# Attention's outputs kept with dimensions on partitions: square sums by a matmul with ones, roots in rows

## The chip, the cores and the metric

The kernel runs on one core of a Trainium2 chip. The metric is device time in microseconds of one execution. A core has TensorE (PE, matmuls; PEld is its weight load), VectorE (DVE), ScalarE (ACT), GpSimd (POOL) and SyncE (SP), which here issues nearly all DMAs. Matmuls read on-chip memory of 128 partitions and write PSUM, eight banks of 128 x 512 words.

## The reference

One block of a hybrid decoder on x (1 x 1024 x 1024): a norm, one combined projection, two groups of heads side by side, an output projection added to x, a last norm.

```python
h = rmsnorm(x, norm1_w)
proj = h @ w_in                       # 4104 columns: sb_q k v z (512 each), g_q k v z (512 each), g_b, g_a
o_sb = stick_breaking_attention(q, k, v)          # 8 heads of 64
o_sb = rmsnorm(o_sb, sb_norm_w) * silu(sb_z)      # a norm per head and position
o_gdn = gated_delta_chunked(gq, gk, gv, decay, beta)  # 4 heads of 128, a scan over chunks
o_gdn = rmsnorm(o_gdn, gdn_norm_w) * silu(g_z)
x = x + concat([o_sb, o_gdn]) @ w_out
out = rmsnorm(x, final_norm_w)
```

Stick-breaking attention gives key s the weight sigmoid(z_ts) times the product of (1 - sigmoid(z_tj)) over the keys j between s and t. So each row needs a scan. What matters here is the line of `o_sb`: every head's 64 outputs at a position are scaled by one over the root of their mean square, and by a gate.

## The kernel before

Products in float32 are made of float32r parts: a high part, and a low part that holds the rest. A product is then three matmuls (`mm3`, line 586).

The work is written as streams, Python generators that issue instructions (`Stream`, line 426, and `interleave`, line 440). While the program is built, a planner with a cost for each kind of instruction plays the streams forward and fixes the order of every engine: TensorE runs the instructions in the order in which the streams issued them, and the other engines in the order in which the planner saw them ready, by priority. So the order on the chip is fixed; an instruction that is late holds up what stands behind it on its engine. A stream gives way at every `yield`; yielding an instruction waits for it in the plan, yielding a function waits until it is true.

Streams by priority on TensorE: the delta rule (`delta_scan`, `delta_solve`, `delta_substitute`, `delta_pre`), the preparation and the weights of the output products, the attention windows, and as filling the projections (priority 100) and the output products.

- **Projections** (line 885). `ORDER`, line 29, is their order: G0 to G3 are a delta head's three projections (k, q, v), k0 to k3 keys of two attention heads each, z0 to z3 the gates of attention, z4 to z7 those of the delta heads, v1 values. Each projection is two halves of 24 matmuls of 512 columns. Its weights come by two loads, are split by ACT and POOL, and the result is evacuated by ACT and DVE and stored to DRAM. Gates and keys have their dimensions on partitions and positions along the row.
- **Delta rule** (lines 960 to 1248). Heads follow one another. A head's pre-stage needs its projections from DRAM, POOL substitutes forward, TensorE finishes the inverse with narrow matmuls (32 and 64 columns of weights), and the scan runs over eight chunks. It ends with the scale factors `rsg`. When the last is there, the weights of the output projection are loaded (line 1388).
- **Attention** (lines 1254 to 1363). For each of eight heads there are four windows of 256 positions (`window`, line 1287): scores, sigmoids on ACT, a scan on DVE, a product on POOL, transposes, and the weighted values into the bank `po`. This bank holds 128 rows by 256 positions: rows 0 to 63 come from the values' high parts, 64 to 127 from their low parts. ACT copies it to `o2`, two transposes put positions on partitions, a DVE reduction adds both halves, and the 256 x 64 outputs go to `o_s`, positions first. In the profile o2 appears as `o2f` and `otf`.
- **Output products** (lines 1404 to 1562). `enter_delta` and `enter_attention` load a block of 128 positions and its gates (`mgf`) and apply the norms. For attention this means a square on ACT, a reduction and a scaling on DVE, a root on POOL, and a multiplication. `prepare` and `split` transpose the block (four transposes, `mwf`), multiply it by the gates and split it into `mh` and `ml`. `products_delta` and then `products_attention` run 24 matmuls or more a block; the last also makes the final norm and stores.

Of the kernel before, what the change touches and what calls it, by code (L numbers as in the profile page):

```python
# [473 lines left out]
def block(tc, xT_d, x_d, n1_d, wE_d, wQ_d, wC_d, conv_d, alog_d, dtb_d, mixw_d, wo_d, fnw_d, out_d):  # L474
# [4 lines left out]
    with ExitStack() as top:  # L479
# [6 lines left out]

        fx = Fixed(ck, nc, {**{f"sg{w}": (2048 * (w + 1), 1) for w in range(4)}, "o2": (1024, 1), "kq": (4096, 4)})
        cst = open_pool("cst")
# [41 lines left out]
        g_s = dr.tile([GH, 3, P, T], F32, name="g_s")  # L530
        o_s = dr.tile([NB, P, 512], F32, name="o_s")
        og_s = dr.tile([NB, P, GH, P], F32, name="og_s")
# [14 lines left out]
        s0 = open_pool("s0", ctx=s0_ctx)  # L547
        n1 = s0.tile([P, NK], F32, name="n1")
        rbc = s0.tile([P, T], F32, name="rbc")
# [11 lines left out]
        class Columns:  # L561
# [629 lines left out]
        def gdn_chain(h, g):  # L1191
# [7 lines left out]
            for j in range(4):  # L1199
# [3 lines left out]
                if c == 0:  # L1203
                    xc = nkv[:, 0, :]
                else:
                    TE.matmul(ks, kq[:, j, 0, :], s_prev, start=True, stop=True)
                    xc = gd.tile([P, P], F32, tag="xct", bufs=2, name="xct")
                    yield V.scalar_tensor_tensor(xc, ks, gsc["neg"][:, h, c:c + 1], nkv[:, j, :], ALU.mult, ALU.add)
# [3 lines left out]
                if c < NB - 1:  # L1212
                    v2 = gd.tile([P, P], F32, tag="v2", bufs=2, name="v2")
                    r = V.tensor_scalar(v2, tx, r2k[:, j:j + 1], None, ALU.mult)
# [72 lines left out]
        def window(h, w, tok):  # L1287
# [30 lines left out]
            for j in range(w + 2):  # L1318
# [44 lines left out]
            yield  # L1363
# [43 lines left out]

        def split(pool, mg, gt):
            tp = pz()
            mw = fx.words(mg, "mw")  # L1410
            yield from turned(tp, [mw[:, 0, j * P:(j + 1) * P] for j in range(4)])
            fv = pools[0].tile([P, 512], F32, tag="mf", name="mf")
            V.tensor_tensor(fv, tp, gt.rearrange("p k t -> p (k t)"), ALU.mult)
            ck.free(mg)
            mh, ml = [pool.tile([P, 4, P], F32R, tag=f"m{c}", bufs=3, name=f"m{c}") for c in "hl"]
            A.activation(mh.rearrange("p k t -> p (k t)"), fv, AF.Copy)
            r = G.tensor_tensor(ml.rearrange("p k t -> p (k t)"), fv, mh.rearrange("p k t -> p (k t)").bitcast(F32), ALU.subtract)
            ck.hold(mh, ml)
            return mh, ml, r
# [32 lines left out]
        def prepare(g):  # L1452
            for b in range(NB):
                yield lambda: ("in", b, g) in ready and (b < 3 or f"{'ad'[g]}{b - 3}" in flags) and (b > 2 or g or f"d{5 + b}" in flags)
                mg, gt, r = ready["in", b, g]
                yield r
                yield lambda: ps.room("pz", 4)
                ready[b, g] = yield from split(pools[0], mg, gt)
                yield
# [20 lines left out]
        def products_delta():  # L1480
            for b in range(NB):
                for got in product(b, 1, (slice(0, 512), slice(512, D))):
# [8 lines left out]
                    yield  # L1491

        def enter_attention():
            yield lambda: "pool1" in flags and "z3" in flags and 3 in wts
            f0, f1 = pools[0], pools[1]
            for b in range(NB):
                yield lambda: f"e{SBH - 1}{b // 2}" in flags and ("in", NB - 1, 1) in ready and fx.room("kq")
# [12 lines left out]
                ready["in", b, 0] = mg, gt, V.tensor_tensor(o, o, rs.unsqueeze(2).to_broadcast([P, SBH, SBD]), ALU.mult)  # L1510
                yield

        def products_attention():
            yield lambda: f"d{NB - 1}" in flags
            for b in range(NB):
# [3 lines left out]
                for got in product(b, 0, parts):  # L1519
# [7 lines left out]
                    V.tensor_tensor(y[:, hs], yp, y[:, hs], ALU.add)  # L1527
                    junk = pools[1].tile([P, 568], F32, tag="yj", name="yj")
                    if n == 2:
# [39 lines left out]
                    Stream(enter_delta(), 9.3, OUTPUT), Stream(prepare(1), 9.2, OUTPUT), Stream(products_delta(), 101, OUTPUT),  # L1569
                    Stream(enter_attention(), 9.1, OUTPUT - 3), Stream(prepare(0), 9.05, OUTPUT - 2), Stream(products_attention(), 102, OUTPUT - 1.5)])  # L1570

# [37 lines left out]
```

## Time and profile before

| | |
|---|---|
| median of 3 runs | 647.9 us (647.87 to 647.94) |
| profiled execution | 648.05 us |
| its span | 646.3 us |
| TensorE busy, granted clock | 637.6 us, 0.998 |
| DVE, ACT, POOL busy | 425.0, 394.1, 339.3 us |
| DMA | 111.82 MB, mean 173 GB/s |

The profile is one execution. Its busy shares are averages over stages: up to about 85 us the first projections, then attention, delta rule and projections side by side up to about 546, then output products. Matmuls overlap their ends, so the distance between the starts of two neighbours, and not the duration of one, is what a matmul takes. All instructions are recorded through one helper and have its line, L358; they are told apart by the names of their tiles.

### The profile page before, as it was taken

How to read it: one execution, taken by the hardware profiler on the slowest of the kernel's cores; microseconds unless marked ns; L12 is line 12 of the kernel's file. 1: busy time of each engine (PE TensorE's matmuls, PEld its weight loads, DVE VectorE, ACT ScalarE, POOL GpSimd, SP SyncE). 2: the span in 40 equal slices, each digit the busy share in tenths (PEclk: the TensorE clock that was granted, in tenths of full speed). 3: DMA queues.
4: the chain of work that ended last, by engine and by line, in shares of the span. 5: the costliest groups of instructions: out<-in, count | busy, mean ns of one | idle time of the engine just before them, and what ended most of it. 6: DMA issues, size and time to landing. Idle time of an engine off the chain costs nothing.

```text
span 646.3 us, 11666 instructions
## 1 busy us (share of the span) xinstructions
PE 637.6 (99%) x3976; PEld 549.7 (85%) x3976; DVE 425.0 (66%) x779; ACT 394.1 (61%) x945; POOL 339.3 (53%) x428
## 2 busy tenths in 40 slices
PE   8999999999999999999999999999999999999996
PEld 7889988988888898888988888988888887888885
DVE  4469974223897768887658777585774237468864
ACT  5764577724968778787668677586654342132553
POOL 0115056837793668974496955668432232136632
PEclk9999999999999999999999999999999999999999
DMA  8886338866472553654345733636222279773123
GB/s 298 323 280 227 132 118 284 275 201 211 140 228 86 159 182 93 218 160 144 118 148 141 244 110 121 203 101 190 85 62 86 83 244 320 287 227 99 65 102 126
DMA packets 96666, 111.82 MB, mean 173 GB/s; under 512 B 28576, under 2 KB 61536, under 8 KB 96608
## 3 DMA queue, kind: packets, MB, share of 16 engines
q1 hardware_dynamic: 96320, 110.89, 53.0%
q8 instruction: 31, 0.51, 0.3%
q14 instruction: 27, 0.22, 0.1%
q10 hardware_dynamic: 288, 0.20, 0.1%
HBM read 76.03 MB, written 35.03 MB: 172 GB/s over the span
## 4 chain that ended last, share of the span: by engine, by line
PE 94%; DVE 2%; ACT 1%; issue 1%; POOL 1%; DMA 1%; POOLq 0%; SPq 0%; DVEq 0%; ACTq 0%
PE pp L358 55%; PE pz L358 27%; PE po L358 8%; PE pc L358 3%; DVE mgf L358 1%; POOL rsb L358 1%; DMA mgf<-gate_s 0%; DVE ssb L358 0%; DVE xr L358 0%; DVE mf L358 0%; ACT xinv L358 0%; ACT sgf L358 0%; DMA xr<-x 0%; DVE wol L358 0%; ACT nkv L358 0%
## 5 line engine op out<-in xcount | busy, mean ns | idle before, releaser
L358 PE MATMUL pp<-xh,weh 128*128 128x512 f32 x360 | 147.9, 411 | 0.0
L358 PE MATMUL pp<-xh,wel 128*128 128x512 f32 x360 | 141.5, 393 | 0.0
L358 PE MATMUL pp<-xl,weh 128*128 128x512 f32 x360 | 140.8, 391 | 0.0
L358 POOL TENSOR_TENSOR sgf<-sgf,cc 128x128 f32<-128x128 f32 (+3 forms) x64 | 77.3, 1210 | 56.8 <-DVE cc L358 52.5
L358 POOL TENSOR_TENSOR wel<-wer,weh 128x512 fp32r<-128x512 f32 x48 | 62.5, 1305 | 74.5 <-ACT weh L358 71.7
L358 PEld LDWEIGHTS pp<-xh,wel 128*128 128x128 f32 x360 | 67.6, 188 | 15.3
L358 PEld LDWEIGHTS pp<-xl,weh 128*128 128x128 f32 x360 | 67.8, 188 | 10.8
L358 PEld LDWEIGHTS pp<-xh,weh 128*128 128x128 f32 x360 | 67.6, 188 | 10.9 <-DVE ac L358 0.2
L358 DVE TENSOR_TENSOR_SCAN cc<-pz,step 128x384 f32<-128x384 f32 (+2 forms) x64 | 53.6, 848 | 13.1 <-ACT pz L358 9.5
L358 DVE TENSOR_TENSOR al<-pz,ah 128x512 fp32r<-128x512 f32 (+1 forms) x80 | 49.7, 632 | 18.9 <-ACT ah L358 18.5
L358 ACT ACTIVATE ah<-pz 128x512 fp32r<-128x512 f32 (+1 forms) x80 | 43.7, 565 | 24.1 <-PE pz L358 23.8
L358 ACT ACTIVATE sgf<-pz,rs 128x384 f32<-128x384 f32 (+3 forms) x96 | 54.5, 600 | 4.9 <-PE pz L358 4.6
L358 ACT ACTIVATE pz<-pz,ns 128x384 f32<-128x384 f32 (+3 forms) x96 | 53.2, 583 | 0.0
L358 PE MATMUL pp<-woh,mh 128*128 128x512 f32 (+2 forms) x132 | 51.9, 393 | 0.6 <-DMA mgf<-gate_s 0.5
L358 PE MATMUL pp<-woh,ml 128*128 128x512 f32 (+2 forms) x132 | 50.9, 385 | 0.0
L358 PE MATMUL pp<-wol,mh 128*128 128x512 f32 (+2 forms) x132 | 50.6, 384 | 0.0
L358 PE MATMUL po<-ah,v2a 128*128 128x256 f32 (+1 forms) x160 | 43.9, 300 | 0.0
L358 POOL TENSOR_TENSOR ml<-mf,mh 128x512 fp32r<-128x512 f32 x16 | 21.6, 1348 | 42.3 <-ACT mh L358 37.7
L358 DVE TENSOR_TENSOR_SCAN cc<-pz,cc,step 128x512 f32<-128x512 f32 (+1 forms) x32 | 38.8, 1213 | 6.7 <-ACT pz L358 5.8
L358 POOL TENSOR_TENSOR ac<-ac,pre 128x512 f32<-128x512 f32 x24 | 31.1, 1294 | 19.1 <-ACT pre L358 12.9
L358 DVE SCALAR_TENSOR_TENSOR pp<-pre,conv,pp 128x512 f32<-128x512 f32 x42 | 31.5, 751 | 13.6 <-ACT pp L358 13.0
L358 PE MATMUL po<-al,v2a 128*128 128x256 f32 (+1 forms) x160 | 38.7, 280 | 0.0
(292 smaller groups left out, 1591.5 us busy)
## 6 DMA issues: line engine op xcount, KB each, us to landing
wer<-wE SPq DMA_DIRECT2D x48, 256.0 KB, 3.6
xr<-x SPq DMA_DIRECT2D x16, 512.0 KB, 7.2
g_s<-ac SPq DMA_DIRECT2D x24, 256.0 KB, 2.4
v_s<-v2e SPq DMA_DIRECT2D x16, 256.0 KB, 2.4
kqf<-g_s SPq DMA_DIRECT2D x16, 256.0 KB, 3.5
v2a<-v_s SPq DMA_DIRECT2D x8, 512.0 KB, 4.3
q<-qk_s SPq DMA_DIRECT2D x8, 512.0 KB, 5.2
kh<-qk_s SPq DMA_DIRECT2D x8, 512.0 KB, 4.9
```

The source lines that it names most:

```text
L358: ins = f(*args, **kw).ins
```

## The change

A window no longer transposes its outputs. ACT copies the lower half of the bank (the low parts' share) to 64 partitions of `o2`, DVE adds the upper half, and the sum, 64 dimensions by 256 positions, is stored as it is. ACT squares it, the squares are split into a float32r high part and a rest on the other 64 partitions (ACT, POOL), and one matmul with a column of ones adds all 128 rows: the head's square sums in one row, which DVE copies and SP stores to `ss_s`.

A new stream, `attention_norms`, loads all sums as 64 rows of 128, makes one over the root on DVE (`_rsqrt`, line 48), and stores them to `rn_s`. `enter_attention` loads outputs and gates with dimensions on partitions, and each head's factors broadcast over its 64 partitions by two loads, and multiplies the gates by them. `split` does not transpose attention's blocks any more: it multiplies outputs by gates directly.

The order of projections becomes "... k1 k2 G2 G3 z4 k3 z5 ..." instead of "... k1 G2 k2 G3 k3 z4 z5 ...". Some buffers are made smaller (`xct`, `v2`, `junk`), `o2` gets a second one, `n1` is padded, and a column of ones is made at the start on ACT.

```diff
-ORDER = "G0 v1 k0 G1 k1 G2 k2 G3 k3 z4 z5 z6 z7 z0 z1 z2 z3".split()
+ORDER = "G0 v1 k0 G1 k1 k2 G2 G3 z4 k3 z5 z6 z7 z0 z1 z2 z3".split()
...
+        oner = cst.tile([P, 1], F32R, name="oner")
+        nc.scalar.activation(oner, half[:, 0:1], AF.Copy, scale=-2.0)
...
+            ts = slice(256 * w, 256 * w + 256)
+            yield lambda: fx.room("o2")
             o2 = fx.tile([P, 256], F32, "o2", "o2")
-            yield A.activation(o2, ov[:, 0:256], AF.Copy)
+            ck.hold(o2)
+            up, o = o2[0:64], o2[64:128]
+            A.activation(up, ov[64:128, 0:256], AF.Copy)
+            yield V.tensor_tensor(o, ov[0:64, 0:256], up, ALU.add)
             busy["po"] = 0
-            op = pz()
-            ot = fx.words(o2, "ot")
-            for i in range(2):
-                TE.transpose(op[:, i * P:(i + 1) * P].bitcast(F32R), ot[:, i * P:(i + 1) * P], idr)
-            oe = at_.tile([P, 2, SBD], F32, tag="oe", bufs=2, name="oe")
-            V.tensor_reduce(oe, op[:, 0:256].rearrange("p (i u d) -> p i d u", i=2, u=2), AX.X, ALU.add)
-            flags[f"e{h}{w}"] = S.dma_start(o_s[2 * w:2 * w + 2, :, h * SBD:(h + 1) * SBD].rearrange("b t d -> t b d"), oe)
+            A.activation(up, o, AF.Square)
+            yield lambda: at_.room("oe", 1)
+            sq = at_.tile([P, 256], F32R, tag="oe", name="sq")
+            ck.hold(sq)
+            A.activation(sq[0:64], up, AF.Copy)
+            r = G.tensor_tensor(sq[64:128], up, sq[0:64].bitcast(F32), ALU.subtract)
+            S.dma_start(o_s[h // 2, (h % 2) * 64:(h % 2) * 64 + 64, ts], o)
+            yield r
+            sp = pz()
+            TE.matmul(sp[0:1, 0:256], oner, sq, start=True, stop=True)
+            V.tensor_copy(o2[0:1], sp[0:1, 0:256])
+            flags[f"e{h}{w}"] = S.dma_start(ss_s[h:h + 1, ts], o2[0:1])
+            ck.free(o2, sq)
...
-        def split(pool, mg, gt):
-            tp = pz()
-            mw = fx.words(mg, "mw")
-            yield from turned(tp, [mw[:, 0, j * P:(j + 1) * P] for j in range(4)])
+        def split(pool, mg, gt, g):
             fv = pools[0].tile([P, 512], F32, tag="mf", name="mf")
-            V.tensor_tensor(fv, tp, gt.rearrange("p k t -> p (k t)"), ALU.mult)
+            if g:
+                tp = pz()
+                mw = fx.words(mg, "mw")
+                yield from turned(tp, [mw[:, 0, j * P:(j + 1) * P] for j in range(4)])
+                V.tensor_tensor(fv, tp, gt.rearrange("p k t -> p (k t)"), ALU.mult)
+            else:
+                V.tensor_tensor(fv, mg[:, 0, :], mg[:, 1, :], ALU.mult)
...
+        def attention_norms():
+            yield lambda: "pool0" in flags and all(f"e{SBH - 1}{w}" in flags for w in range(4))
+            nt = pools[0].tile([P, 3, P], F32, tag="sq", name="nt")
+            nv, rn, un = [nt[0:64, n, :] for n in range(3)]
+            S.dma_start(nv, ss_s.rearrange("h (b t) -> (h b) t", b=NB))
+            V.tensor_scalar(nv, nv, 1.0 / SBD, EPS, ALU.mult, ALU.add)
+            _rsqrt(V, None, rn, nv, P, un)
+            flags["rn"] = S.dma_start(rn_s.rearrange("h (b t) -> (h b) t", b=NB), rn)
...
-                S.dma_start(mx, o_s[b])
+                S.dma_start(mx.rearrange("p (k t) -> p k t", k=4), o_s[:, :, bs].rearrange("k p t -> p k t"))
                 ck.hold(mg)
-                S.dma_start(gt, gate_s[0:4, :, b * P:(b + 1) * P].rearrange("k e t -> e k t"))
-                o = mx.rearrange("p (h d) -> p h d", d=SBD)
-                sq = f0.tile([P, 512], F32, tag="sq", name="sq")
-                A.activation(sq, mx, AF.Square)
-                ss = f0.tile([P, SBH], F32, tag="ssb", name="ssb")
-                V.tensor_reduce(ss, sq.rearrange("p (h d) -> p h d", d=SBD), AX.X, ALU.add)
-                rs = f0.tile([P, SBH], F32, tag="rsb", name="rsb")
-                V.tensor_scalar(ss, ss, 1.0 / SBD, EPS, ALU.mult, ALU.add)
-                rsqrt(rs, ss, SBH)
-                ready["in", b, 0] = mg, gt, V.tensor_tensor(o, o, rs.unsqueeze(2).to_broadcast([P, SBH, SBD]), ALU.mult)
+                S.dma_start(gt, gate_s[0:4, :, bs].rearrange("k e t -> e k t"))
+                rb = f1.tile([P, 4, P], F32, tag="wr", bufs=2, name="rb")
+                for u in range(2):
+                    S.dma_start(rb[64 * u:64 * u + 64], rn_s.rearrange("(k u) t -> u k t", u=2)[u, :, bs].partition_broadcast(64))
+                ready["in", b, 0] = mg, gt, V.tensor_tensor(gt, gt, rb, ALU.mult)
```

More of the change, by code (lines that the diff above doesn't have):

```diff
@@ L485, in open_pool @@
             return Pool(ck, ctx.enter_context(tc.tile_pool(name=name, bufs=1, **kw)), space, before)
-        fx = Fixed(ck, nc, {**{f"sg{w}": (2048 * (w + 1), 1) for w in range(4)}, "o2": (1024, 1), "kq": (4096, 4)})
+        fx = Fixed(ck, nc, {**{f"sg{w}": (2048 * (w + 1), 1) for w in range(4)}, "o2": (1024, 2), "kq": (4096, 4)})
         cst = open_pool("cst")
@@ L530, in block @@
         g_s = dr.tile([GH, 3, P, T], F32, name="g_s")
-        o_s = dr.tile([NB, P, 512], F32, name="o_s")
+        o_s = dr.tile([SBH // 2, P, T], F32, name="o_s")
+        ss_s = dr.tile([SBH, T], F32, name="ss_s")
+        rn_s = dr.tile([SBH, T], F32, name="rn_s")
         og_s = dr.tile([NB, P, GH, P], F32, name="og_s")
@@ L547, in block @@
         s0 = open_pool("s0", ctx=s0_ctx)
-        n1 = s0.tile([P, NK], F32, name="n1")
+        n1 = s0.tile([P, 64], F32, name="n1")[:, 0:NK]
         rbc = s0.tile([P, T], F32, name="rbc")
@@ L1206, in gdn_chain @@
                     TE.matmul(ks, kq[:, j, 0, :], s_prev, start=True, stop=True)
-                    xc = gd.tile([P, P], F32, tag="xct", bufs=2, name="xct")
+                    xc = gd.tile([P, P], F32, tag="xct", bufs=1, name="xct")
                     yield V.scalar_tensor_tensor(xc, ks, gsc["neg"][:, h, c:c + 1], nkv[:, j, :], ALU.mult, ALU.add)
@@ L1212, in gdn_chain @@
                 if c < NB - 1:
-                    v2 = gd.tile([P, P], F32, tag="v2", bufs=2, name="v2")
+                    v2 = gd.tile([P, P], F32, tag="v2", bufs=1, name="v2")
                     r = V.tensor_scalar(v2, tx, r2k[:, j:j + 1], None, ALU.mult)
@@ L1455, in prepare @@
                 mg, gt, r = ready["in", b, g]
-                yield r
-                yield lambda: ps.room("pz", 4)
-                ready[b, g] = yield from split(pools[0], mg, gt)
+                if g:
+                    yield r
+                    yield lambda: ps.room("pz", 4)
+                ready[b, g] = yield from split(pools[0], mg, gt, g)
                 yield
@@ L1495, in enter_attention @@
             f0, f1 = pools[0], pools[1]
+            yield lambda: "rn" in flags
             for b in range(NB):
-                yield lambda: f"e{SBH - 1}{b // 2}" in flags and ("in", NB - 1, 1) in ready and fx.room("kq")
+                yield lambda: ("in", NB - 1, 1) in ready and fx.room("kq")
+                bs = slice(b * P, (b + 1) * P)
                 mg, mx, gt = block_inputs()
-                S.dma_start(mx, o_s[b])
+                S.dma_start(mx.rearrange("p (k t) -> p k t", k=4), o_s[:, :, bs].rearrange("k p t -> p k t"))
                 ck.hold(mg)
-                S.dma_start(gt, gate_s[0:4, :, b * P:(b + 1) * P].rearrange("k e t -> e k t"))
-                o = mx.rearrange("p (h d) -> p h d", d=SBD)
-                sq = f0.tile([P, 512], F32, tag="sq", name="sq")
-                A.activation(sq, mx, AF.Square)
-                ss = f0.tile([P, SBH], F32, tag="ssb", name="ssb")
-                V.tensor_reduce(ss, sq.rearrange("p (h d) -> p h d", d=SBD), AX.X, ALU.add)
-                rs = f0.tile([P, SBH], F32, tag="rsb", name="rsb")
-                V.tensor_scalar(ss, ss, 1.0 / SBD, EPS, ALU.mult, ALU.add)
-                rsqrt(rs, ss, SBH)
-                ready["in", b, 0] = mg, gt, V.tensor_tensor(o, o, rs.unsqueeze(2).to_broadcast([P, SBH, SBD]), ALU.mult)
+                S.dma_start(gt, gate_s[0:4, :, bs].rearrange("k e t -> e k t"))
[3 more added lines that the diff above has]
+                ready["in", b, 0] = mg, gt, V.tensor_tensor(gt, gt, rb, ALU.mult)
                 yield
@@ L1527, in products_attention @@
                     V.tensor_tensor(y[:, hs], yp, y[:, hs], ALU.add)
-                    junk = pools[1].tile([P, 568], F32, tag="yj", name="yj")
+                    junk = pools[1].tile([P, 560], F32, tag="yj", name="yj")
                     if n == 2:
```

3 lines of the change are left out of this document (2 added, 1 removed).

## The prediction

> **What bounds the kernel now.** I read the page's busy table and the chain of waits first, then TensorE's waits, then the busy time by stretches.
>
> ```profile
> PE 637.6 (99%) x3976; PEld 549.7 (85%) x3976; DVE 425.0 (66%) x779; ACT 394.1 (61%) x945; POOL 339.3 (53%) x428
> PE 94%; DVE 2%; ACT 1%; issue 1%; POOL 1%; DMA 1%; POOLq 0%; SPq 0%; DVEq 0%; ACTq 0%
> PE pp L358 <- DMA mgf<-gate_s: 0.5, 1, 0.5
> PE pz L358 <- DVE al L358: 0.2, 1, 0.2
> 165.00:500.00 335.00, 334.71 (x2386) 290.46 (x2385) 248.95 (x450) 241.15 (x648) 217.86 (x286) 1.00 0.48 144
> 500.00:546.00 46.00, 46.00 (x229) 38.47 (x227) 19.49 (x39) 16.73 (x35) 13.55 (x14) 1.00 0.66 217
> 546.00:640.00 94.00, 93.44 (x450) 76.96 (x448) 64.13 (x112) 38.25 (x73) 37.77 (x31) 1.00 0.45 153
> ```
>
> The first line is each engine's busy time, the second the chain by engine: TensorE is both the busiest engine and the path. The two waits are all that the profile shows of it standing still after the start. The last three rows are stretches (length, then busy time of PE, weight load, DVE, ACT, POOL): attention beside the delta rule and the projections, the end of the projections, the output products. TensorE fills 334.71 of 335, 46 of 46 and 93.44 of 94 us. The program's TensorE order is fixed when it is built, and other engines have room. So I count the change in TensorE time, start to start, and ask of everything else only whether it is still covered.
>
> **Removed from TensorE: 64 transposes in the windows.** Timeline of TensorE, start and duration of one (durations overlap; only the distance of starts is cost):
>
> ```profile
> 175.12 0.29 PE L358 MATMUL pz<-step,otf 128*128 128x128 f32 x2
> 175.25 0.35 PE L358 MATMUL po<-ah,v2a 128*128 128x256 f32 x1
> 175.44 0.28 PE L358 MATMUL po<-al,v2a 128*128 128x256 f32 x1
> 175.55 0.28 PE L358 MATMUL po<-ah,v2a 128*128 128x256 f32 x1
> ```
>
> The two take 0.13 us (175.25 - 175.12), and the matmul behind them 0.19 instead of the 0.11 of its neighbour: 0.21 us a window. Eight heads by four windows are 32: 32 x 0.21 = 6.7 us.
>
> **Removed: attention's transposes ahead of the output products**, four a block in eight blocks (the delta heads keep theirs):
>
> ```profile
> 593.35 0.46 PE L358 MATMUL pz<-step,mwf 128*128 128x128 f32 x4
> 593.64 0.46 PE L358 MATMUL pp<-woh,mh 128*128 128x512 f32 x1
> 593.94 0.39 PE L358 MATMUL pp<-wol,mh 128*128 128x512 f32 x1
> 594.17 0.40 PE L358 MATMUL pp<-woh,ml 128*128 128x512 f32 x1
> ```
>
> Four take 0.29, the next 0.30 instead of 0.23: 0.36 us a block, 8 x 0.36 = 2.9 us. Together 9.6 us go.
>
> **Added: 32 matmuls with ones.** Each has one column of weights and 256 moving columns. Streaming them costs about 0.12, between the neighbours 0.11 (175.44 to 175.55 above) and 0.13. What else it costs is the question of this prediction. No matmul of before has one column. The nearest that multiply are 64 columns wide:
>
> ```profile
> 470.47 0.40 PE L358 MATMUL pz<-kh,q 128*128 128x512 f32 x1
> 470.71 0.39 PE L358 MATMUL pz<-kl,q 128*128 128x512 f32 x1
> 471.02 1.15 PE L358 MATMUL pz<-xinv,wy 128*64 128x64 f32 x16
> 472.10 0.50 PE L358 MATMUL pp<-xh,weh 128*128 128x512 f32 x1
> 472.44 0.40 PE L358 MATMUL pp<-xl,weh 128*128 128x512 f32 x1
> ```
>
> The full-width matmul ahead of the narrow group lasts 0.31 start to start where its like lasts 0.24 (470.47 to 470.71): TensorE runs empty before the narrow ones begin, 0.07 to 0.08. The first full-width matmul behind lasts 0.34 instead of 0.23: 0.11. The emptying on the way out is hidden in the row of 16; an estimate is the same 0.08. So 0.12 + 0.08 + 0.08 + 0.11 = 0.39 us each, 32 x 0.39 = 12.5 us. The other end is the one narrow operation that entered free:
>
> ```profile
> 95.00 0.39 PE L358 MATMUL pz<-xh,wel 128*128 128x512 f32 x1
> 95.23 0.27 PE L358 MATMUL pz<-step,cum 128*32 128x128 f32 x1
> 95.34 0.27 PE L358 MATMUL pz<-step,eg 128*32 128x128 f32 x1
> 95.37 0.47 PE L358 MATMUL pp<-xh,weh 128*128 128x512 f32 x1
> 95.68 0.39 PE L358 MATMUL pp<-xl,weh 128*128 128x512 f32 x1
> ```
>
> Here the matmul ahead keeps 0.23 and only the one behind pays 0.08 (0.31). By it a sum costs 0.12 to 0.20, 3.8 to 6.4 us in all. But these two are transposes, which the first case shows to cost 0.08 behind them at full width too; the sum with ones multiplies, so I take the 64-wide row. The break-even is 9.6 / 32 = 0.30 us a sum. The upper end, for weights that load late on both sides, is 0.50 (16 us).
>
> The Trainium skill, TensorEngine Tiling (Array Packing), Key Properties, says that changing the tiling mode, not just the tile, drains TensorE. The 0.07 at 470.71 agrees; the free entry at 95.23 does not show it. By that rule the sums cost the 12.5 us, without it 3.8.
>
> **What becomes of the wait at the changeover.**
>
> ```profile
> 545.94 0.39 PE L358 MATMUL pp<-xh,wel 128*128 128x512 f32 x1
> 546.79 0.47 PE L358 MATMUL pp<-woh,mh 128*128 128x512 f32 x1 [0.46 <-DMA mgf<-gate_s]
> ```
>
> The first output product comes 0.85 after the last projection, 0.62 more than a matmul takes: the first delta block is late. With 32 x (0.39 - 0.21) = 5.8 us more TensorE work ahead, the loads have that cover and the 0.6 goes. Were the sums cheap, the windows would end 2.9 us sooner, and this wait could grow by as much.
>
> **Other engines in the windows.** The nearest rows for old and new work:
>
> ```profile
> L358 ACT ACTIVATE o2f<-po 128x256 f32<-128x256 f32 x32 | 12.5, 390 | 15.3 <-PE po L358 12.9 <-PE pz L358 2.1
> L358 DVE TENSOR_REDUCE oe<-pz 128x128 f32<-128x256 f32 x32 | 13.3, 416 | 2.0 <-PE pz L358 1.6
> L358 DVE TENSOR_TENSOR at<-pz,dt 128x256 f32<-128x256 f32 x16 | 6.4, 413 | 2.4 <-PE pz L358 2.4
> L358 POOL TENSOR_TENSOR sgf<-sgf,cc 128x256 f32<-128x256 f32 x8 | 5.1, 643 | 2.2 <-DVE cc L358 2.1
> ```
>
> A window's ACT work goes from one operation of 0.39 to three, +0.78; DVE from a reduction (0.42) to an addition and a one-row copy (0.41 each), +0.41; POOL gains a subtraction of 0.64. Times 32: ACT +25, DVE +13, POOL +21 us, which in the 335 us stretch makes 266, 262 and 238: none reaches TensorE. The bank of the weighted values is now free after ACT and DVE instead of ACT alone, 0.4 later, and the window also waits for one of two output slots, for a place for the squares, and for POOL before its sum. Behind the sum on TensorE lie projections; behind the subtraction on POOL the weights' splits and the sigmoid products; behind the second, 1 KB store on SP the weight loads. Those follow in the order planned, which puts a sum behind its inputs. If each window ended 1.8 us later (ACT, DVE, POOL together), attention would end 32 x 1.8 = 58 us later at worst. Its cover is 74 us: last store issued at 496.5, first use at 570.2.
>
> ```profile
> L358 SPq DMA_DIRECT2D o_s<-oe x32: 360/378/1067, 176.1 to 496.5; - x32
> L358 SPq DMA_DIRECT2D mgf<-o_s x8: 319/320/628, 570.2 to 601.0; - x8
> 445.67 1.03 POOL L358 TENSOR_TENSOR rsg<-sso,half 128x4 f32<-128x4 f32 x1
> 478.81 0.29 DVE L358 COPY state<-pz 128x128 f32<-128x128 f32 x1 [0.20 <-PE pz L358]
> mgf<-gate_s SPq DMA_DIRECT2D x16, 256.0 KB, 5.8
> ```
>
> I price the windows' other work at nothing; if the cover is gone, the output products of attention start late, by what is beyond 74.
>
> **Roots and gates.** The root chain is eleven DVE operations of 128 columns, under 0.41 each, so under 4.5 us, and a load and a store; it lies between the last window and 570. A block of attention loses a square, a reduction, a scaling and POOL's root and gains one multiplication and two broadcast loads. Sixteen loads more on SP at 0.3 to 0.4 are 6 us of issue, and loads of the gates land in 5.8, while TensorE spends 5.5 a block. Price nothing: DVE and POOL are shorter there, and TensorE's 93.44 of 94 leaves 0.56 to win at most.
>
> **Order of projections.** G2 moves behind k2, and k3 behind z4; each move puts one projection of 48 matmuls, 48 x 0.23 = 11 us of TensorE, with its two weight loads, splits, evacuations and stores, ahead on every queue. G3 stands behind the same steps as before. Delta head 2 may so end 11 to 17 us later than 445.7, still before head 3's first state at 478.8; k3 delays attention's heads 6 and 7 by some 11 to 17 us, which with nothing else lies inside the 74. Price nothing, bounds 0 and 11. The smaller buffers are free: each is written again only a chunk later.
>
> **Start.** A column of ones is made on ACT:
>
> ```profile
> 0.79 0.41 ACTq L631 DMA_DIRECT2D n<-n  x1
> 1.23 1.28 ACT L358 ACT_TABLE_LOAD   x1 [1.23 <-PEq L1584]
> 3.82 0.72 ACT L358 ACTIVATE xh<-xr0f,n 128x512 fp32r<-128x512 f32 x1 [1.08 <-DMA n<-n]
> ```
>
> ACT waits 1.08 for the gain, whose load ACT itself issues. If the column were made ahead of that load, table and column, 1.5 us, would delay the start as much; behind it they fall into the wait. It needs a DVE result while the load needs nothing, so I take behind: nothing, bounds 0 and 1.5.
>
> **Sum.** -6.7 - 2.9 + 12.5 - 0.6 = +2.3 us. The profiled execution took 648.05 us, its span 646.3 and 1.75 around it, and stands 0.15 above the median of 647.9. Forecast 650.3, 0.4% slower.
>
> **Rivals.** *The sums stay cheap (faster).* TensorE does not empty for them; for it speaks the free entry at 95.23, against it the 64-wide row. -9.6 + 3.8 = -5.8, of which up to 2.9 may go into the wait at 546: 642.1 to 645.0, about 643.5. It decides below 0.30 us a sum. The Trainium skill, TensorE: Matmul & The Clock Gate, Step-by-step: what each phase is for, has weight loads pulled ahead of running matmuls; with a column as short as this that speaks for this rival, and no row here shows it for one column. *Nothing measurable:* part of the emptying overlaps and a sum costs near 0.30: 647 to 649. *The new order starves the delta rule:* head 2's delay passes on to head 3 and to the last scale factors, and the changeover at 546 waits for it, up to 11 us: 654 to 661. Against it stand the 33 us between 445.7 and 478.8.
>
> **How the numbers follow.** Forecast 0.53 (its own range 649 to 654), cheap sums 0.25, nothing 0.14, starved 0.08. About 0.2%, 1.3 us, is what a measurement tells from no change. Faster 0.25, same 0.14, slower 0.53 + 0.08 = 0.61. The range, 643 to 655, leaves out the lower part of the cheap case (about 0.08) and most of the starved one.
>
> **What would show it.** Right: a group of 32 sums with the matmul ahead of each at about 0.31 start to start and the one behind at about 0.34; 32 instead of 64 transposes ahead of the output products; no wait at the changeover; TensorE at 99%. Wrong: 0.23 around the sums, a longer wait for the gates at the changeover, holes in TensorE between 400 and 570, or a first matmul later than before.

## The result: 650.5 us, 0.4% slower, and the profile after

The changed kernel takes 650.46 us (median of 6 runs, 649.84 to 651.74) where the kernel before, beside it on the same chip, takes 647.92: a ratio of 1.0039, interval 1.0028 to 1.0049. The forecast of 650.3 holds the number. The trace shows that it comes about in another way than I said. In the order of the prediction, first the page of the changed kernel (busy time by engine), with its profiled execution of 651.44 us and a span of 649.7. This execution is 1.0 us above the median; a stretch in which TensorE was granted half its clock, worth 1.6 us, is in it, and not every execution has one:

```profile
PE 636.1 (98%) x3912; PEld 544.9 (84%) x3912; DVE 436.1 (67%) x806; ACT 417.7 (64%) x1002; POOL 350.1 (54%) x452
```

TensorE's busy time has fallen, from 637.6 to 636.1 us, and yet the span is 3.4 us longer. So TensorE did less and stood still more, or ran slower. The same three stretches as before (length, then busy time of PE, weight load, DVE, ACT, POOL, the granted clock, DMA share, GB/s):

```profile
165.00:500.00 335.00, 332.11 (x2326) 285.26 (x2325) 261.20 (x474) 265.06 (x699) 240.16 (x315) 1.00 0.48 144
500.00:546.00 46.00, 46.00 (x248) 39.21 (x247) 23.69 (x56) 20.76 (x48) 13.69 (x15) 1.00 0.60 196
546.00:640.00 94.00, 91.56 (x405) 74.51 (x404) 56.91 (x94) 32.01 (x61) 24.31 (x23) 0.98 0.61 185
```

TensorE lacks 2.9 us in the first stretch (0.3 before) and 2.4 in the last (0.6 before), where its clock is 0.98 instead of 1.00 too. DVE, ACT and POOL in the first stretch stand at 261, 265 and 240, almost exactly the 262, 266 and 238 that the prediction had counted. Their sizes were right; the sentence that followed, "none reaches TensorE", was not. TensorE's waits (total, times, longest), of which the first row belongs to the output products and the others to the windows:

```profile
PE pp L358 <- DVE xr L358: 2.4, 3, 1.9
...
PE pz L358 <- DVE al L358: 1.2, 2, 0.8
PE pz L358 <- DVE cc L358: 0.7, 2, 0.6
PE pz L358 <- POOL sq L358: 0.2, 1, 0.2
```

Now the sums themselves, by TensorE's timeline. This one stands between full-width matmuls, so its whole price can be read:

```profile
381.65 0.40 PE L358 MATMUL pp<-xh,wel 128*128 128x512 f32 x1
381.88 0.28 PE L358 MATMUL pz<-sq,oner 128*1 128x256 f32 x1
382.00 0.39 PE L358 MATMUL pp<-xh,weh 128*128 128x512 f32 x1
382.23 0.40 PE L358 MATMUL pp<-xl,weh 128*128 128x512 f32 x1
```

The matmul ahead keeps its 0.23 us, the sum takes 0.12, the one behind 0.23. The prediction wanted 0.31 and 0.34 around it. Nothing runs empty: a sum costs the streaming of its columns. Where sums follow the delta rule's matmuls, 0.20 goes by from their start to the next (the two transposes of before took 0.20 there too). 32 sums cost 3.8 to 6.4 us, not 12.5; the distances from each to the next matmul add up to 5.8, a few short waits included. Two transposes had taken as much themselves (0.13 and 0.20 in the same places), so what a window saves is the 0.08 of the matmul behind them.

The changeover has no wait, as forecast, but it comes late:

```profile
548.44 0.39 PE L358 MATMUL pp<-xh,wel 128*128 128x512 f32 x1
548.67 0.39 PE L358 MATMUL pp<-woh,mh 128*128 128x512 f32 x1
```

For an account I summed, over the matmul records, the distance between two starts beyond the streaming of the first one's columns (0.23 us for 512), where more than 0.13 is over; I call these holes. A matmul of 512 columns at half clock counts too, with 0.20. From 165 us to the changeover there are 4.2 us of them before and 8.4 after; behind 600 us 0.3 before and 4.5 after.

- Up to the first output product: -6.7 for the transposes, +3.8 to +6.4 for the sums, -0.6 for the wait, should give 543.3 to 545.9. It starts at 548.67 (546.79 before). 2.8 to 5.4 us went; the holes grew by 4.2.
- From there to the last matmul: 94.3 us (548.67 to 642.98) where before needs 93.1 (546.79 to 639.93) and 2.9 us of transposes have gone. 4.1 us went; the holes grew by 4.2, of which 1.6 are matmuls at half clock (below).

So the change saves TensorE time, and more is given back, in two places. What the place behind 600 us looks like on DVE:

```profile
601.02 0.69 DVE L358 TENSOR_TENSOR mgf<-mgf,rb 128x512 f32<-128x512 f32 x1 [3.11 <-DMA mgf<-gate_s]
...
608.53 0.69 DVE L358 TENSOR_TENSOR mgf<-mgf,rb 128x512 f32<-128x512 f32 x1 [1.86 <-DMA rb<-rn_s]
609.14 0.68 DVE L358 TENSOR_TENSOR xr<-po,fnw 128x512 f32<-128x512 f32 x1
609.74 0.68 DVE L358 TENSOR_TENSOR mf<-mgf 128x512 f32<-128x512 f32 x1
610.34 0.68 DVE L358 TENSOR_TENSOR xr<-pp,xr 128x512 f32<-128x512 f32 x1
```

and on TensorE:

```profile
608.83 0.39 PE L358 MATMUL pp<-woh,ml 128*128 128x512 f32 x1
611.07 0.50 PE L358 MATMUL pp<-woh,mh 128*128 128x512 f32 x1 [1.86 <-DVE xr L358]
...
612.34 0.60 PE L358 MATMUL pp<-woh,ml 128*128 128x512 f32 x1
612.74 0.63 PE L358 MATMUL pp<-woh,mh 128*128 128x512 f32 x1
613.17 0.63 PE L358 MATMUL pp<-wol,mh 128*128 128x512 f32 x1
...
615.73 0.42 PE L358 MATMUL pp<-wol,mh 128*128 128x512 f32 x1
615.99 0.39 PE L358 MATMUL pp<-woh,ml 128*128 128x512 f32 x1
```

DVE stands 1.86 us before the multiplication of gates by factors, because the broadcast load of the factors has not landed. Behind it, in DVE's fixed order, stands the addition `xr<-pp` that frees the bank TensorE wants next. TensorE waits the same 1.86 (611.07). And then it runs slow: from 612.34 to 615.73 a matmul of 512 columns takes 0.43 us instead of 0.23. That makes 1.6 of the 4.5 us of holes behind 600. The multiplication at 601.02 waited 3.11 us for the gates' load, not the factors'. The factors that come late at 608.53 were loaded from 601.74 on, right behind that multiplication; they have two buffers, and whether a third would help is not tried here.

### The profile page after: what moved, and what is told of

Read it like the earlier page. It is cut to its first block, busy times and chain, and to the rows that moved or that the text cites. A ratio compares the mean times of both kernels' runs of the same rounds, so it can differ in the third digit from the quotient of the medians.

```text
span 649.7 us, 11808 instructions
## 1 busy us (share of the span) xinstructions
PE 636.1 (98%) x3912; PEld 544.9 (84%) x3912; DVE 436.1 (67%) x806; ACT 417.7 (64%) x1002; POOL 350.1 (54%) x452
## 5 line engine op out<-in xcount | busy, mean ns | idle before, releaser
L358 ACT ACTIVATE sgf<-pz,rs 128x384 f32<-128x384 f32 (+3 forms) x96 | 53.1, 587 | 1.6 <-PE pz L358 1.3
L358 ACT ACTIVATE pz<-pz,ns 128x384 f32<-128x384 f32 (+3 forms) x96 | 51.9, 566 | 0.2
L358 PE MATMUL po<-ah,v2a 128*128 128x256 f32 (+1 forms) x160 | 42.0, 289 | 0.0
```

What stands on the lines that cost most here:

```text
L358: ins = f(*args, **kw).ins
```

## The experiments

Two theories for each question. For the sums: narrow weights empty TensorE (on record), or something else in the rows from which I priced them did. For the end: the place of the wait on DVE, or the number of small packets, or the loads simply coming too late. For the holes before 546 us: the length of the windows' added work, or the order of projections and the plan.

### Is it the broadcast loads? e1_once

```diff
-                rb = f1.tile([P, 4, P], F32, tag="wr", bufs=2, name="rb")
-                for u in range(2):
-                    S.dma_start(rb[64 * u:64 * u + 64], rn_s...partition_broadcast(64))
+                if b == 0:
+                    rb = ...   # loaded once, held, used for all eight blocks
```

> Edit: the broadcast factors are loaded for block 0 only and used for all eight blocks (so blocks 1 to 7 get block 0's factors); 14 of the 16 broadcast loads go, everything else stays. Theory A (the sums are cheap, as the trace after shows, and the gain is given back by holes: about 4.2 us in the output products, where DVE waits for broadcast loads with the evacuations behind it, and the rest while attention runs): 646.3, 645 to 647.5, no TensorE wait for DVE xr after 595. Theory B (the new order of projections eats the gain): no change, 650 to 651. Theory C (the sums cost 0.39 us each after all): no change, 650 to 651.

Measured: 647.38 us, ratio 0.9993 (0.9984 to 1.0003), 3 us less than the changed kernel and inside theory A's range. No hole is left behind 546 us; from the first output product to the last matmul it takes 89.6 us (548.74 to 638.3) instead of 94.3. That is 3.6 below before, where the four removed transposes a block promised 2.9. So the loads of the factors cost all that was lost at the end. How they cost it is not told by this run.

### The two orders of projections: e2_old_order, e3_before_new_order

```diff
-ORDER = "G0 v1 k0 G1 k1 k2 G2 G3 z4 k3 z5 z6 z7 z0 z1 z2 z3".split()
+ORDER = "G0 v1 k0 G1 k1 G2 k2 G3 k3 z4 z5 z6 z7 z0 z1 z2 z3".split()
```

for the first; the reverse, in the kernel before, for the second.

> Edit: the changed kernel with the order of projections of before. Theory A: 650.5 within 1 us, since the holes come from loads and engines and not from the order. Theory B: 645 to 647, the gain of the removed transposes comes out. Theory C: 650.5 within 1 us.

> Edit: the kernel before with the new order of projections alone. Theory A: 647.9 within 1 us. Theory B: 651 to 654, and the changeover to the output products waits longer than the 0.62 us of before. Theory C: 647.9 within 1 us.

Measured: 652.86 us (1.0073, 1.0060 to 1.0085) and 654.93 (1.0103, 1.0087 to 1.0118). No theory has both: A and C wanted no change in either, and B wanted a gain in the first, which lost, and 651 to 654 in the second, which took a little more. Each kernel is slower with the other's order: the changed one by 2.2 us beyond its 1.0039, the kernel before by 6.7. So the order is neither a gain nor a loss by itself; it goes with the windows. In the changed kernel with the old order TensorE's longest wait is for POOL, by its timeline:

```profile
280.15 2.51 POOL L358 TENSOR_TENSOR wel<-wer,weh 128x512 fp32r<-128x512 f32 x2
...
281.48 0.19 PEld L358 LDWEIGHTS pp<-xh,wel 128*128 128x128 f32 x1 [3.42 <-POOL wel L358]
281.48 0.50 PE L358 MATMUL pp<-xh,wel 128*128 128x512 f32 x1 [2.99 <-POOL wel L358]
```

A weight's low part, made on POOL, comes 3 us late. This is the queue to which the change added 0.73 us a window. That this work makes it late is not shown: the kernel before in the new order, which has none of it, waits 1.7 us for the same part.

### Does a wider column cost more? e4_wide64

```diff
-            TE.matmul(sp[0:1, 0:256], oner, sq, start=True, stop=True)
+            TE.matmul(sp[0:64, 0:256], idr[:, 0:64], sq, start=True, stop=True)
```

The weights are 64 columns of the identity, so the row that is stored holds no sum. Only the shape counts.

> Edit: the 32 sum matmuls take 64 columns of the identity as weights in place of one column of ones (so the square sums are left out, a single square stands in their place). If 64 columns make TensorE empty itself as the float32 matmuls of the delta rule do, each sum costs 0.27 us more, 32 x 0.27 = 8.6 us: 656 to 660, with the matmul ahead at 0.31 start to start. If the emptying belongs to those float32 matmuls and not to the width: 650.5 within 1 us. Theory C expects 650.5 too, since the narrow mode would already be paid.

Measured: 650.8 us (1.0037, 1.0024 to 1.0051). The same place on TensorE's timeline:

```profile
381.67 0.40 PE L358 MATMUL pp<-xh,wel 128*128 128x512 f32 x1
381.90 0.28 PE L358 MATMUL pz<-sq,step 128*64 128x256 f32 x1
382.02 0.39 PE L358 MATMUL pp<-xh,weh 128*128 128x512 f32 x1
382.25 0.40 PE L358 MATMUL pp<-xl,weh 128*128 128x512 f32 x1
```

0.23, 0.12, 0.23 again, with as many columns as the row of 64 from which the prediction took its emptying. So the width alone is not it. That row differs from these in other ways too: it is sixteen matmuls of 64 moving columns, and its operands are float32, where these are float32r. The next run changes the type.

### The type of the sums: e10_float32_sums

```diff
-        oner = cst.tile([P, 1], F32R, name="oner")
+        oner = cst.tile([P, 1], F32, name="oner")
...
-            sq = at_.tile([P, 256], F32R, tag="oe", name="sq")
+            sq = at_.tile([P, 256], F32, tag="oe", name="sq")
```

The planner counts the sum as before, so all engines keep the order of the changed kernel.

> The instruction order of after (650.46) on every engine; only the type of the squares and of the column of ones is float32 instead of float32r, as in the 64-wide rows from which the sum was priced. Theory (the emptying of TensorE that the prediction took from those rows belongs to float32, not to the narrow tile): the matmul ahead of a sum takes 0.31 instead of 0.23 or the one behind 0.31 to 0.34, the sum itself 0.21 (float32, 256 columns: 0.215 in the rows of kqf): 32 x (0.10 + 0.08 to 0.19) = 5.8 to 9.3 us more, 656 to 660. Rival (no emptying for float32 either, only two passes): 32 x 0.10 = 3.2 us more, 653 to 654.5.

Measured: 663.6 us (1.0238, 1.0224 to 1.0252). The same sum, on TensorE's timeline:

```profile
388.06 0.39 PE L358 MATMUL pp<-xl,weh 128*128 128x512 f32 x1
388.29 0.40 PE L358 MATMUL pp<-xh,wel 128*128 128x512 f32 x1
388.62 0.59 PE L358 MATMUL pz<-sq,oner 128*1 128x256 f32 x2
389.14 0.50 PE L358 MATMUL pp<-xh,weh 128*128 128x512 f32 x1
389.48 0.40 PE L358 MATMUL pp<-xl,weh 128*128 128x512 f32 x1
```

Ahead 0.33, behind 0.34: the two marks that the prediction had named, to the hundredth or two, and they appear when the type changes and nothing else. So the emptying that I read in the 64-wide rows does not come with a narrow tile by itself. Nor does it come with float32 by itself. The kernel before has float32 matmuls at full width, on TensorE's timeline:

```profile
514.37 0.40 PE L358 MATMUL pp<-xh,wel 128*128 128x512 f32 x1
514.61 0.38 PE L358 MATMUL pc<-xct,xinv 128*128 128x128 f32 x2
...
515.19 0.48 PE L358 MATMUL pp<-xh,weh 128*128 128x512 f32 x1
515.51 0.40 PE L358 MATMUL pp<-xl,weh 128*128 128x512 f32 x1
```

The matmul ahead takes 0.24, as without them; only the one behind pays (0.32). By its matmul records a matmul of 512 columns takes 0.23 to 0.24 ahead of 78 of 79 such full-width float32 groups (0.31 once), and 0.32 or more ahead of all 13 narrow ones of the delta rule. So it takes both, float32 and narrow weights, and these rows were there before the prediction. My expectation missed the size: the sum takes 0.52, not 0.21, because it runs as two matmuls (x2), and the 0.215 of the row that I used was one of two. The first output product comes 13.7 us later than in the changed kernel (562.35). The sums' own distances add up to 16.7 instead of 5.8, and those of the matmuls around them grow by 5.9; 3.1 of this does not arrive: TensorE waits less elsewhere, for DVE al and cc together 0.9 us instead of 1.9.

The Trainium skill, TensorEngine Tiling (Array Packing), Key Properties, has a change of the tiling mode drain TensorE. By that rule the narrow sums should have been emptied for in float32r as well; no run here shows that, at 1 or at 64 columns (0.23 ahead, 0.23 behind), and float32 shows it at 1 column (0.33 ahead) and not at full width (0.24). Here the measurement decides: the rule shows in float32 alone.

### Small packets, or the place of the wait? e6_pairs, e7_factor_on_pool, e8_later_in_plan

e6 loads the factors of two blocks at once, 8 loads with rows of 1 KB instead of 16 with rows of 512 B:

```diff
-                rb = f1.tile([P, 4, P], F32, tag="wr", bufs=2, name="rb")
+                if b % 2 == 0:
+                    rb = f1.tile([P, 4, 2 * P], F32, tag="wr", bufs=2, name="rb")
```

e7 moves the multiplication to POOL:

```diff
-                ready["in", b, 0] = mg, gt, V.tensor_tensor(gt, gt, rb, ALU.mult)
+                ready["in", b, 0] = mg, gt, G.tensor_tensor(gt, gt, rb, ALU.mult)
```

e8 tells the planner that these loads land 3 us later than it thinks, and changes nothing else:

```diff
-            self.at(self.dma + 1500, self.finish, op)
+            self.at(self.dma + 1500 + op.late_by, self.finish, op)
...
+            op.late_by = 3000 if self.eng == "S" and outs[0].tensor.name.startswith("rb_") else 0
```

> The broadcast factors are loaded for two blocks at a time: 8 loads of 1 KB rows instead of 16 of 512 B rows, all else as in after (650.46). Theory A1 (the many small packets make the loads of gates and factors land late: 13149 packets in 565 to 610 us against 5955 before, DMA engines 67.7% busy against 45.4%): about half the added packets go, the 4.5 us of tail holes shrink by half or more, 647 to 649. Rival A2 (it is the wait's place, in VectorE's queue ahead of the evacuations, that costs, and a larger load lands no sooner): 650 or up to 1 us above.

> One word: the multiplication of gates by factors goes from VectorE to POOL, loads unchanged. Theory A2 (VectorE waits in order for the load while finished output products stand behind it in PSUM): TensorE's holes of 0.6 to 2.3 us after 600 go, 646.5 to 648.0. Rival A1 (the loads simply land too late for the blocks): the wait only moves from VectorE to POOL and from there to the products, 649.5 to 651.5.

> The planner is told that the factor loads land 3 us later than it thought; only the order of instructions changes. Theory A2 with its cause in the plan (the plan put the multiplication 3 us too early among the evacuations): the holes after 600 shrink, 647 to 649. Rival A1: 650 to 651, the products wait for late data whatever the order.

| | us | ratio | output products, first start to last | holes behind 600 us |
|---|---|---|---|---|
| before | 648.0 | 1 | 93.1 | 0.3 |
| changed | 650.46 | 1.0039 | 94.3 | 4.5 (1.6 at half clock) |
| e1, one load for all | 647.38 | 0.9993 (0.9984 to 1.0003) | 89.6 | 0 |
| e6, pairs | 649.34 | 1.0023 (1.0012 to 1.0035) | 91.0 | 1.3 |
| e7, on POOL | 651.37 | 1.0048 (1.0035 to 1.0060) | 95.4 | 5.8 (1.5 at half clock) |
| e8, later in the plan | 646.55 | 0.9979 (0.9970 to 0.9988) | 89.7 | 0 |

The stretch at half clock is not the whole of the loss: the profile of e4, in the changed kernel's order, has none behind 600 us, and it takes 92.6 us for the output products with 2.5 us of holes.

e8 has every load of the changed kernel, its packets (13010 against 13149 between 565 and 610 us, where before has 5955), its buffers and its multiplications, and loses nothing: 89.7 us, as good as without the loads. So neither the packets nor the landing itself was the cost. It was the plan's order, in the first place where it had put the multiplication among DVE's evacuations (ACT's and SP's orders shift a little with it). e8's DVE on its timeline:

```profile
604.20 0.69 DVE L358 TENSOR_TENSOR xr<-pp,xr 128x512 f32<-128x512 f32 x1 [0.54 <-PE pp L358]
604.81 0.68 DVE L358 TENSOR_TENSOR mgf<-mgf,rb 128x512 f32<-128x512 f32 x1
605.40 0.69 DVE L358 TENSOR_TENSOR xr<-pc,fnw 128x512 f32<-128x512 f32 x1
```

The multiplication finds its factors there; one wait of 0.91 is left, at 608.79, that TensorE doesn't feel. e6 lies between the two theories and fits the packets' one in its sign; fewer loads waste less, but DVE still waits for one of them up to 2.4 us. e7 refutes my simplest form of the theory. It clears DVE of the wait and gets worse, because POOL has a fixed order too, by its timeline:

```profile
607.84 1.27 POOL L358 TENSOR_TENSOR mgf<-mgf,rb 128x512 f32<-128x512 f32 x1 [2.02 <-DMA rb<-rn_s]
...
608.53 0.19 PEld L358 LDWEIGHTS pp<-woh,mh 128*128 128x128 f32 x1 [1.68 <-DVE xr L358]
608.53 0.50 PE L358 MATMUL pp<-woh,mh 128*128 128x512 f32 x1 [1.25 <-DVE xr L358]
```

POOL also makes the roots of the last norm. ACT now waits up to 3.6 us for one of them (1.7 in the changed kernel), DVE 11.0 us in all for ACT (2.4), and TensorE for DVE again. The wait is handed on to what stands behind it, on POOL as on DVE.

e8 beats both kernels: 1.4 us below before, 3.9 below the changed one by the two ratios.

### The windows: e5_no_sums, e9_light_windows

e5 leaves square, split, sum, row copy and their store out of the windows, and takes a constant for the sums:

```diff
-            A.activation(up, o, AF.Square)
...
-            TE.matmul(sp[0:1, 0:256], oner, sq, start=True, stop=True)
-            V.tensor_copy(o2[0:1], sp[0:1, 0:256])
-            flags[f"e{h}{w}"] = S.dma_start(ss_s[h:h + 1, ts], o2[0:1])
+            flags[f"e{h}{w}"] = S.dma_start(o_s[...], o)
```

> Leaves out the norms: no square, split, subtraction, sum matmul, row copy or store of sums in the windows; the roots come from a constant and the broadcast factors are loaded once, as in e1_once, which is the kernel to compare with (647.4). Theory W (the holes of TensorE between 165 and 546 us, 8.4 us of stalls above 0.13 us against 4.2 before, come from the windows' longer work on ACT, DVE and POOL): besides 32 sums at 0.12 to 0.18 (3.8 to 5.8 us) some 3 to 4 us of holes go as well: 638 to 640.5. Rival X (the holes come from the changed order of projections and the shared weighted-values bank, not from the square, split and copy): only the sums' own time goes, 641.5 to 643.5. On-record price (0.39 a sum, drains): 647.4 - 12.5 = 635.

The text names the loads wrongly: the kernel as it ran keeps all sixteen factor loads, so it compares with the changed kernel, not with e1. Measured: 650.22 us (1.0033, 1.0021 to 1.0045), no gain at all from 160 operations less. Both theories had wanted some. The last projection does end 7.2 us earlier (541.21 against 548.45), and then TensorE waits:

```profile
541.21 0.39 PE L358 MATMUL pp<-xh,wel 128*128 128x512 f32 x1
543.15 0.50 PE L358 MATMUL pz<-step,mwf 128*128 128x128 f32 x4 [1.55 <-DMA mgf<-gate_s]
...
545.10 0.50 PE L358 MATMUL pp<-woh,mh 128*128 128x512 f32 x1 [1.45 <-ACT mh L358]
...
546.75 0.80 PE L358 MATMUL pp<-woh,ml 128*128 128x512 f32 x1 [0.80 <-POOL ml L358]
```

The planner, with less to place, made another order: the delta rule's last scale factors come at 526.9 instead of 522.1, and the first output block with them. And behind these holes, from 545.56 to 552.38, the granted clock is 0.50. The run shows that taking work away also changes the order, and that here this cost, with the half clock behind it, as much as the work. It does not separate them.

e9 does. It keeps the order of e8 on every engine: the planner counts the added operations in full, but on the chip they work on 32 columns instead of 256.

```diff
+            COST.append(93 + 256 / 1.2)
-            A.activation(up, o, AF.Square)
+            A.activation(up[:, 0:32], o[:, 0:32], AF.Square)
```

and so for the high part, the subtraction, the sum and the row copy.

> The instruction order of e8_later_in_plan (646.55) on every engine, but the windows' added operations (square, high part, subtraction, sum matmul, row copy) work on 32 columns instead of 256, while the planner still counts them at full length; the norms are left out (a constant takes their place). Theory W (the holes of TensorE between 165 and 546 us, 8.4 us, come from the length of the added operations on ACT, DVE and POOL): the holes fall towards the 4.2 us of before, and the sums stream 0.05 to 0.09 less each: 639.5 to 642. Rival X (they come from the order that the planner made, whatever the operations take): only the sums' streaming goes, 1.6 to 2.9 us: 643.5 to 645.

Measured: 642.35 us (0.9908, 0.9893 to 0.9923), 4.2 below e8. The first output product starts at 544.56 instead of 550.21; 1.6 of this is a stretch at half clock that e8's profile has and e9's has not (below), so I take the holes of the changed kernel, which has none ahead of 546, to compare with. The stretch from 165 to 546 us (busy times of PE, weight load, DVE, ACT, POOL) of the kernel before:

```profile
165.00:546.00 381.00, 380.71 (x2613) 328.93 (x2611) 268.44 (x489) 257.88 (x683) 231.41 (x299) 1.00 0.50 153
```

of the changed kernel:

```profile
165.00:546.00 381.00, 378.11 (x2571) 324.47 (x2570) 284.89 (x529) 285.82 (x747) 253.85 (x330) 1.00 0.49 151
```

and of e9:

```profile
165.00:546.00 381.00, 379.33 (x2587) 327.27 (x2586) 278.94 (x533) 275.99 (x749) 240.44 (x331) 1.00 0.49 153
```

Holes: 4.2, 8.4 and 6.1 us. So of the 4.2 that the change added, 2.3 go when the added operations get short, in the same order. The other 1.9 stay with the order, or with what remains of the operations; these runs don't tell. Both theories had a part, and neither its number: theory W asked for 639.5 to 642, the rival for 643.5 to 645. The sums' streaming gives less than the rival wanted (1.6 to 2.9): a sum of 32 columns takes 0.03 (378.67 to 378.70 on e9's timeline), but the matmul behind it takes 0.31 instead of 0.23, and over all 32 both together save 1.2 us.

### Once more another order: e11_z_order

```diff
-ORDER = "G0 v1 k0 G1 k1 k2 G2 G3 z4 k3 z5 z6 z7 z0 z1 z2 z3".split()
+ORDER = "G0 v1 k0 G1 k1 k2 G2 G3 z4 k3 z5 z6 z0 z1 z7 z2 z3".split()
```

on e8.

> e8_later_in_plan with the order of projections changed once more: z0 and z1 ahead of z7; everything ahead of z6's end keeps its place. Theory (with the tail mended, the time is set by how far the planner's order fits): within 1.5 us of 646.55, 645 to 648. Rival (any move of projections costs several us, as the new order cost the kernel before 6.7 us): 649 to 654.

Measured: 646.85 us (0.9987, 0.9976 to 0.9997), the same as e8 within their intervals. This is inside the theory's range. One late move among gates costs nothing here; the exchanges of e2 and e3, which cost 2.2 and 6.7 us, move delta heads and keys as well, whose results other stages wait for. Which of their moves costs is not shown.

## Why the prediction was right in the number and wrong in the reason

- *32 sums at 0.39 us, 12.5 in all.* This step failed, and it was the main one: 0.12 between float32r matmuls, 0.20 behind the delta rule's. The row was real, the reading not. I saw that "narrow" and "emptied" stood together and took the one for the cause; the row differed from the sums in type as well. e10 shows that the type matters, and the full-width float32 rows show that it takes both. The other row that I quoted, the free entry at 95.23, was the better guide, and I argued it away. My rival of cheap sums had the mechanism, and its 642.1 to 645.0 was missed because the gain was given back.
- *64 and 32 transposes removed.* Right in the main: where nothing is lost (e1, e8) the output products take 3.5 us less than before, for which 2.9 stood and 0.3 of holes. The 6.7 of the windows no run measures alone.
- *Other engines in the windows: nothing.* This step failed. The sizes of the work were right, and the cover of 74 us for attention's end held (last store 507.2, first use 572.0). But I had asked only whether the end of attention had cover. DVE's scans and evacuations of the delta rule and of attention stand in the same queues as the new operations, and TensorE waits for them by turns (2.5 us by the profile's waits from 165 to 546 us, 0.2 before): 4.2 us of holes more, of which e9 traces 2.3 to the added work.
- *Roots and gates: nothing.* This step failed. I had written that loads of the gates land in 5.8 us while TensorE spends 5.5 a block, and concluded that 0.56 could be won at most, without asking what could be lost. The 5.8, too, was the median over the loads of both groups of heads; those of attention's blocks landed in 3.4 in the kernel before. The new wait stands on DVE ahead of the evacuations: 4.5 us of holes, 1.6 of them a stretch at half clock behind the longest. e8 shows that it needn't stand there.
- *Order of projections: nothing, bounds 0 and 11.* The shift of delta head 2 (last factors at 464.2 instead of 445.7, 18.5 us later where 11 to 17 stood) did not pass on to head 3 (first state at 480.2, from 478.8), as worked out. But the price is not one number: the new order costs the kernel before 6.7 us, and spares the changed one 2.2.
- *Changeover and start.* Right: 0.23 from the last projection to the first output product, and the column of ones is made behind the gain's load (2.52), with the first `xh` at 3.82 as before.

So +2.3 forecast from one cost that was not there met two that were: 8.4 us more of holes (1.6 of them at half clock) against 3.2 to 5.8 us of TensorE work saved and 0.6 of a wait, which makes +2.0 to +4.6; the spans stand 3.4 apart. That the sum of these came out near +2.3 is luck.

## What to carry to other kernels

When a price is read off a neighbour in the trace, list every way in which the neighbour differs (type, width, what stands around it) before one of them is made the cause; rows of the same trace that have only one of them narrow it down, and a run that changes the one and keeps the order settles it. In a kernel with orders fixed by a plan, a new wait is priced by what stands behind it in that engine's queue, and a plan that believes a load lands early turns its latency into a stall; telling the plan the truth can be worth more than the change. Work on engines with room is free only if none of their other results is awaited in the meantime.

## What was not expected of the hardware

Half clock behind short holes. In the changed kernel matmuls of 512 columns take 0.43 us for 3.4 us, beginning 1.3 us after a hole of 2.0 (rows at 612.34 to 615.73 above). In e8 the same happens at another place, on TensorE's timeline, behind holes of 0.8 and 0.4 us at 399 and 402:

```profile
402.73 0.50 PE L358 MATMUL pp<-xh,weh 128*128 128x512 f32 x1
403.03 0.62 PE L358 MATMUL pp<-xl,weh 128*128 128x512 f32 x1
403.45 0.63 PE L358 MATMUL pp<-xh,wel 128*128 128x512 f32 x1
```

The changed kernel has these same holes (0.7 and 0.4) and no slow stretch there; e4 has one there with the same order. By the stretch from 403 to 407 us, the granted clock is 0.57 in e8 and 1.00 in the changed kernel:

```profile
403.00:407.00 4.00, 4.00 (x12) 3.01 (x10) 2.38 (x5) 0.90 (x3) 3.25 (x2) 0.57 0.00 0
```

It costs 1.6 us (eight matmuls at 0.20 more), so the profiles of one kernel can differ by that much, and one hole's price isn't only its own length. The Trainium skill, TensorE: Matmul & The Clock Gate, Part 1: The HAM clock gate, gives 426.7 ns from start to start at 512 columns for the gated clock, which agrees with the 0.43 here, and has the gate look at windows that run freely, which fits that the same holes bring it in one execution and not in another. That it takes a whole idle window of about 3.4 us, as the page says, no trace here shows: the clock was halved behind holes of 2.0 us and less, and the measurement decides. What is enough to bring it, these runs don't tell.

A float32 sum with one column of weights between float32r matmuls costs 0.1 us on either side beside its own 0.52, in two records; a float32r sum costs its streaming alone (0.12), with 1 column of weights or with 64; float32 at full width costs nothing ahead of it (0.24).
